# RWKV values turned to rows by token: from a run of their own in phase A into the state part's run of the unit before

## The chip, the cores and the metric

One NeuronCore of a Trainium2 chip runs the whole program. The metric is the device time of one execution in microseconds; lower is better. The engines are PE (TensorE), DVE (VectorE), ACT (ScalarE), POOL (GpSimd) and the DMA queue that SP issues to.

## The reference, cut to what matters

The reference is one layer of a hybrid decoder: 4,096 tokens of width 1,024 are normalised and projected once, the columns feed a gated linear attention group (GLA, 4 heads) and an RWKV-7 group (8 heads of size 64), and both outputs go through a gate, one output projection, a residual add and a last norm. The change touches the RWKV group alone:

```
def step(S, inp):                     # S is (value dim, key dim), one per head
    r_t, w_t, k_t, v_t, kk_t, a_t = inp
    sa = einsum('bhvk,bhk->bhv', S, -kk_t)
    S = S * w_t + sa * (kk_t * a_t) + v_t * k_t
    return S, einsum('bhvk,bhk->bhv', S, r_t)
mu, var = mean(y), var(y)             # per head, over its 64 values
y = (y - mu) * rsqrt(var + 64e-5) * ln_w + ln_b
out = (y + sum(r * k * r_k) * v) * silu(rg)
```

The values v_t are a shifted projection of the normalised input.

## The kernel before, in words

The tokens are cut into 8 blocks of 512 (`TB`). A block has four RWKV units, each with two heads, one on partitions 0 to 63 (`lo`) and one on 64 to 127 (`hi`); unit u is heads pair p = u % 4 of block b = u // 4, so there are 32 units. A unit has 8 chunks of 64 tokens (`NC`, `C`).

Work is written as generators (streams) that run side by side while the program is recorded: `stream_a` (projections and phase A of a unit, `rwkv_ab`), `stream_i` (the rest of the inverse of the unit's triangular matrix, `rwkv_i`), `stream_c` (the chain over the chunks and the output, `rwkv_c`), `rwkv_d` (the norm and the gate), and others for x, the weights, GLA and the output projection. Counters in `done` say which unit each has reached. What is recorded is a list of steps with their dependences. `forward` and `backward` (lines 270 to 356) are a list scheduler that runs over them several times with modelled durations, and the best order by its model is then issued. Every engine takes its instructions in that order. All instructions are therefore put on line 477 by the profile, and groups have to be told apart by tile names. The model of PE is `class Array` (lines 139 to 164): how long a matmul holds its tile of the array, and when PE can take the next one.

Most tiles are shared: `lend` (lines 206 to 218) enters a tile into a pool of its kind (PSUM banks; 512-wide f32 tiles in SBUF; and so on), and `settle` gives each use a place after the scheduling. So a name in the profile is that of the tile whose place was used. `bank` is any of 7 shared PSUM banks, `ch` the eighth; the values v may appear under `mgr`, `xr`, `r` or `go`. `c` is `c64` and keeps its name; `W` holds a unit's matrices.

The array can be used as smaller tiles. A matmul with K = 64 and 64 output partitions uses one quadrant, named by its rows (partitions of the inputs) and columns (partitions of the output). A f32 matmul appears in the trace as two MATMUL records with a weight load each, so 16 matmuls are x32.

Three groups of matmuls matter here.

- The **turn** (lines 1006 to 1014, at the end of phase A). v is stored with values on partitions and tokens along the row; `sv` wants tokens on partitions. Per chunk, two matmuls against `c64` (identity less 1/64, so the mean of each head is taken off too) turn the 64 x 64 pieces. Values of `lo` come out on `hi` and the other way round, so they use the two off-diagonal quadrants. 16 matmuls, then two ACT copies from PSUM into `sv`.
- The **chain** (lines 1051 to 1072): per chunk three dependent matmuls with copies between them, in the `ch` bank. Its first step reads `sv`.
- The **state part** of the output (lines 1073 to 1076): per chunk, `Ss` (state before the chunk) against W's third column block, `lo` to `lo` and `hi` to `hi`: the two diagonal quadrants, 16 matmuls. The part from the chunk's own values (lines 1077 to 1079) follows with K = 128 into the same bank.

`banks` holds the free PSUM banks; `need(st, n)` takes n of them for a stream and frees what the stream held.

Of the kernel before, what the change touches and what calls it, by code (L numbers as in the profile page):

```python
# [10 lines left out]
F32 = mybir.dt.float32  # L11
# [9 lines left out]
P = 128  # L21
# [3 lines left out]
C = 64  # L25
# [23 lines left out]
NC = TB // C  # L49
# [4 lines left out]
W_R, W_RK, W_RV, W_RG = 1, 5, 9, 13  # L54
# [29 lines left out]
def hymba_kernel(ctx, tc, xT, wt, wg, wo, wua, gup, pk, ck, out):  # L84
# [3 lines left out]
    NB = NT // TB  # L88

    one = ctx.enter_context(tc.tile_pool(name="one", bufs=1))  # L90
    wp = ctx.enter_context(tc.tile_pool(name="wp", bufs=1))
    big = ctx.enter_context(tc.tile_pool(name="big", bufs=1))
    un = ctx.enter_context(tc.tile_pool(name="un", bufs=1))
    rt = ctx.enter_context(tc.tile_pool(name="rt", bufs=1))
# [44 lines left out]
    class Array:  # L139
# [5 lines left out]
        def put(self, t, d, cols, tiles):  # L145
            r, c, f32 = tiles
            form = (r[1] - r[0], c[1] - c[0])
            q = [(i, j) for i in range(r[0], r[1]) for j in range(c[0], c[1])]
            turn = form != self.form
            t = max([t, self.free] + [self.tile.get(k, 0.0) for k in (self.tile if turn else q)]) + 0.09 * turn  # L150
            w, k = int(t / 3.413), self.clock
            if w > k[0]:
                k[:] = [w, 0.0, w == k[0] + 1 and k[1] >= 3060]
            k[1] += cols
            d *= 1 if k[2] else 2
            full = len(q) == 16
            if full and f32 == 2:
                load = 0.107 * (c[1] - c[0]) / 4
                d = max(0.0, load - self.one) + max(d / 2, load) + d / 2
            for k in q:  # L160
                self.tile[k] = t + (d if full or not f32 else 0.66 * d)
            self.form, self.f32, self.one = form, f32 > 0, d / max(f32, 1)
            self.free = t + (d if full or turn and f32 else d / 2 if f32 and form != (4, 1) else 0.014)
            return t, d

    array = Array()
# [25 lines left out]
    last, turn = [None, 0], [0]  # L192
# [288 lines left out]
    def after(*what):  # L481

        t = 0.0
        for x in what:
            if isinstance(x, tuple):
                r = ring.get((x[0], F32))
                for i in range(x[1] if r else 0):
                    y = r[1][(r[0] + i) % len(r[1])]
                    t = max([t] + [used.get(k, 0.0) for k in parts(y)])
            else:  # L490
                t = max([t] + [ready.get(k, (0.0, ""))[0] for k in parts(x)])
        return t + EL
# [24 lines left out]
    def sb(pool, shape, dt, tag, bufs=1):  # L517

        key = (tag, dt)
        if key not in ring:  # L520
            ring[key] = [0, [pool.tile(shape, dt, tag=f"{tag}_{i}", name=f"{tag}_{i}") for i in range(bufs)]]
        r = ring[key]
        t = r[1][r[0] % len(r[1])]
        r[0] += 1
        return t if pool is one else lend(t)
# [100 lines left out]
    hls = [wot(), wot()]  # L626
    wdr = [dr.tile([2, P, KT, P], F16, tag=f"wdr{i}", name=f"wdr{i}") for i in range(NWT + KT)]
    wgs = sb(one, [P, 2, KT, 32], F16, "wgs")
    scl = sb(one, [P, 40], F32, "scl")
    wosc = sb(one, [P, KT], F32, "wosc")  # L630
    woinv = sb(one, [P, KT], F32, "woinv")
    nwx = sb(one, [P, 10], F32, "nwx")
# [9 lines left out]
    def get_w(i, st="g"):  # L642
        if st != "o":
            got[st] += 1
        if i not in split_done:
            yield lambda: i in split_done
        if i in first:
            return first.pop(i)
        if st == "o":
            if done["W"] < NWT + KT:  # L650
                yield lambda: done["W"] == NWT + KT
            w = wot()
            w = [w[:, 0], w[:, 1]]
        else:
            w = pair(st)
        for a in range(2):
            D.dma_start(w[a], wdr[i][a])
        return w
# [182 lines left out]
    def proj(w, xs, st="g", kt=KT):  # L841
        yield after(w[0], xs[STEP - 1])
        ps = yield from need(st)
        for n, (a, c) in enumerate(((0, 0), (0, 1), (1, 0))):
            for k in range(kt):
                if k % STEP == 0 and n + k > 0:
                    yield after(w[a], xs[min(k + STEP, kt) - 1])
                count[st] += 1
                T.matmul(ps, lhsT=w[a][:, k, :], rhs=xs[k][:, c, :], start=(n == 0 and k == 0), stop=(n == 2 and k == kt - 1))
        return ps  # L850

    def shift(ps, j, o):

        a = sb(rt, [P, TB + 1], F32, "sa", NSA)
        S.copy(a[:, 0:1], carry[:, j:j + 1])
        S.activation(a[:, 1:TB + 1], ps, AF.Copy, scale=mu_s[:, j:j + 1])
        V.scalar_tensor_tensor(o, ps, omu_s[:, j:j + 1], a[:, 0:TB], ALU.mult, ALU.add)
        rel("r")
        S.copy(carry[:, j:j + 1], a[:, TB:TB + 1])
        return o  # L860
# [29 lines left out]
    def rwkv_ab(u, p, b, xs, LR):  # L890
# [11 lines left out]
        E = tA("E")  # L902
# [75 lines left out]
            D.dma_start(nb[32 * q:32 * q + 32, :, 32 * q:32 * q + 32],  # L978
                              td[:, :, NC * q:NC * q + NC].rearrange("m g c i -> (m g) c i"))

        v = shift((yield from proj((yield from get_w(W_RV + p, "r")), xs, "r")), 8 + p, tA("E"))
        yield lambda: done["C"] >= u - 1
        i = W_RG + p
        pg = yield from proj((yield from get_w(i, "r")), xs, "r")
# [4 lines left out]
        yield after(r)  # L989
        pst = yield from need("r")  # L990
        stat_mm(pst, bones, r)
        brow = sb(rt, [P, P], F32, "brow", 1)
        S.copy(brow, pst[:, 0:P])
        bv = tA("bv", 2)
        bcast(brow, 2, bv, "b")
# [7 lines left out]
        for i in range(2):  # L1003
            S.copy(bk[:, 4 * i:4 * i + 4, :], f4(pt[i]))
        rel("r")
        yield after(v)
        sv = sb(un, [P, NC, 2, 64], F32, "sv", 2)
        pv = (yield from need("r")).rearrange("p (c t) -> p c t", c=NC)
        for c in range(NC):
            t_ = slice(C * c, C * c + C)  # L1010
            T.matmul(pv[64:128, c, :], lhsT=v[0:64, t_], rhs=c64[0:64, :], start=True, stop=True)
            T.matmul(pv[0:64, c, :], lhsT=v[64:128, t_], rhs=c64[64:128, :], start=True, stop=True)
        S.copy(sv[64:128, :, 0, :], pv[64:128])
        S.copy(sv[0:64, :, 1, :], pv[0:64])
        units[u] = (W, nb, sv, bk, PC, bv, tg)
        done["A"] += 1

    def rwkv_i(nb):
# [20 lines left out]
            S.copy(nb[q0:q0 + 32, :, q0 + 32:q0 + 64], pl[q0:q0 + 32, 1])  # L1039
        rel("i")  # L1040

    def rwkv_c(p, b, mgt, st_):
        W, nb, sv, bkt, PC, bv, tg = st_
        yield after(nb, bkt, sv)

        st = Sst[p]
        S.copy(sv[lo, 0, 0, :], st[lo])
        V.tensor_copy(sv[hi, 0, 1, :], st[hi])
        S.copy(Ss[:, 0, :], st)
        dd = ((lo, 0), (hi, 1))  # L1050
        for c in range(NC):
            pc = pbank("ch").rearrange("p (a t) -> p a t", a=8)
            T.matmul(pc[:, 0:2, :], lhsT=W[:, c, 0:2, :].rearrange("p a t -> p (a t)"), rhs=sv[:, c], start=True, stop=True)
            us = sb(rt, [P, 64], F32, "us", 2)
            for q_, e in dd:
                S.copy(us[q_], pc[q_, e, :])
            if c > 0:
                for q_, e in dd:
                    S.copy(Ss[q_, c, :], sv[q_, c, e, :])
            psd = sb(rt, [P, 64], F32, "psd", 2)  # L1060
            yield after(us) + XL
            T.matmul(pc[:, 2, :], lhsT=nb[:, c, :], rhs=us, start=True, stop=True)
            for q_, e in dd:
                S.copy(sv[q_, c, e, :], pc[q_, 2, :])
            S.activation(psd, Ss[:, c, :], AF.Copy, scale=PC[:, c])
            yield after(sv) + XL
            T.matmul(pc[:, 4:6, :], lhsT=bkt[:, c, :], rhs=sv[:, c], start=True, stop=True)
            for q_, e in dd:
                dst = sv[q_, c + 1, e, :] if c < NC - 1 else st[q_]
                V.scalar_tensor_tensor(dst, pc[q_, 4 + e, :], PC[q_, c], psd[q_], ALU.mult, ALU.add)  # L1070
            if c < NC - 1:
                yield after(sv, ("ch", 1)) + XL
        py = (yield from need("y")).rearrange("p (c t) -> p c t", c=NC)
        for c in range(NC):
            for q_, e in dd:
                T.matmul(py[q_, c, :], lhsT=Ss[q_, c, :], rhs=W[q_, c, 2, :], start=c == 0, stop=False)
        for c in range(NC):
            for q_, e in dd:
                T.matmul(py[q_, c, :], lhsT=sv[:, c, e, :], rhs=W[:, c, 5 + e, :], start=False, stop=c == NC - 1)
        yield lambda: done["C"] == done["CC"]  # L1080
        y = sb(rt, [P, TB], F32, "cy")
        rs = sb(rt, [P, TB], F32, "crs")
        S.copy(y, py.rearrange("p c t -> p (c t)"))
        rel("y")
        S.activation(rs, y, AF.Square)
        done["CC"] += 1
        spawn(rwkv_d(p, b, mgt, y, rs, bv, tg), 2.5)
# [281 lines left out]
            D.dma_start(out[P * n:P * n + P, TB * b:TB * b + TB], part[n])  # L1369
        yield now[0]  # L1370

    done = dict.fromkeys(("A", "C", "G", "GE", "GV", "GG", "GH", "I", "CC", "O", "X", "W", "SU", "N"), 0)


    def norm_weight():
# [37 lines left out]
        D.dma_start(c64, ck[:, CK_C64:CK_C64 + 64])  # L1413


    units, hot = {}, []
    mgts = [[None] * KT + [sb(one, [P, KT], F32, f"mxs{b % 3}")] for b in range(NB)]

    def masks():
# [53 lines left out]

    def stream_c():
        for u in range(4 * NB):
            yield lambda: done["I"] > u
            yield from rwkv_c(u % 4, u // 4, mgts[u // 4], units.pop(u))

    def stream_p():
        for b in range(NB):  # L1480
# [110 lines left out]
```

## Time and profile before

| what | value |
|---|---|
| median of 3 runs | 2293.01 us (2292.14 to 2295.88) |
| the profiled execution | 2296.0 us |
| its span, first to last instruction | 2294.2 us |
| mean granted clock of TensorE | 0.99 |
| PE busy | 2219.4 us (97%), 20,200 MATMUL records |
| DVE, ACT, POOL busy | 1714.6, 1312.8, 893.2 us |
| HBM traffic | 276.97 MB read, 45.05 MB written |

Busy time of PE counts every record's modelled duration, overlapping ones once. For a run of small matmuls, the distance from its start to the start of the next row of the timeline is what it takes from PE. The queries used below are the page, the table by stretches of time (`windows`: length of the stretch, then busy time and instructions of PE, weight loads, DVE, ACT and POOL, then the granted clock, the share of DMA and GB/s), the groups of instructions with their shapes, and the timeline (start, length, engine, line, operation, output <- inputs, K*M of the array tile, output shape, records).

### The profile page before, as it was taken

The numbers are of one execution on the slowest core, as the hardware profiler recorded it, in microseconds if no ns is written. First come the engines' busy times: TensorE is split into PE (matmuls) and PEld (weight loads), VectorE is DVE, ScalarE is ACT, GpSimd is POOL, SyncE is SP. The second block draws the span as 40 slices with busy tenths as digits, with TensorE's granted clock in tenths as the row PEclk, the third lists the DMA queues.
The fourth block names the chain that finished last, engine by engine and source line by source line (L and its number), as shares of the span: only waits on it lengthen the run. The fifth ranks groups of instructions, "written<-read, shape, count | busy, mean of one in ns | idle before, by whom it ended". The sixth has DMA issues, their size and how long they took to land.

```text
span 2294.2 us, 54076 instructions
## 1 busy us (share of the span) xinstructions
PE 2219.4 (97%) x20200; PEld 1370.0 (60%) x20200; DVE 1714.6 (75%) x3863; ACT 1312.8 (57%) x3605; POOL 893.2 (39%) x2219
## 2 busy tenths in 40 slices
PE   6989999899999999999999999999999999999997
PEld 2546576456655666556665566655666566755663
DVE  8868979758685877777776596776877596776876
ACT  6657776555655546455663656555475464644562
POOL 4422534462155440554417253345315544044400
PEclk9999999999999999999999999999999999999998
DMA  7586454635444543456435344344534544344432
GB/s 248 184 239 209 129 180 147 182 106 164 124 129 141 158 139 107 118 154 182 117 101 167 101 158 131 109 132 131 170 103 133 168 132 134 112 119 117 114 116 70
DMA packets 275516, 325.59 MB, mean 142 GB/s; under 512 B 131716, under 2 KB 132916, under 8 KB 275252
## 3 DMA queue, kind: packets, MB, share of 16 engines
q1 hardware_dynamic: 275252, 322.13, 47.3%
q8 instruction: 158, 2.59, 0.5%
q14 instruction: 106, 0.87, 0.1%
HBM read 276.97 MB, written 45.05 MB: 140 GB/s over the span
## 4 chain that ended last, share of the span: by engine, by line
PE 79%; DVE 11%; DMA 5%; ACT 2%; issue 2%; POOL 1%; SPq 1%; DVEq 0%; ACTq 0%; POOLq 0%
PE bank L477 71%; PE ch L477 7%; DVE W L477 1%; DMA wdr<-wo 1%; DVE x L477 1%; DVE mgg L477 1%; POOL Tc L477 1%; SPq L477 1%; DVE mgr L477 1%; POOL tm L477 1%; DVE sv L477 1%; DMA x<-in_wt_dram 0%; ACT wo L477 0%; DMA mgg<-in_xT_dram 0%; DVE rgs L477 0%
## 5 line engine op out<-in xcount | busy, mean ns | idle before, releaser
L477 PE MATMUL bank<-x,wr 128*128 128x512 f16 x2992 | 758.3, 382 | 10.5 <-ACT x L477 4.6
L477 PE MATMUL bank<-x,wg 128*128 128x512 f16 x1808 | 466.3, 383 | 6.9 <-DVE wg L477 3.4
L477 PEld LDWEIGHTS <-wr 128*128 128x128 f16 x2992 | 290.6, 100 | 281.6 <-issue 21.5
L477 POOL TENSOR_TENSOR Tc<-Tc,tm 128x60 f32<-128x60 f32 (+24 forms) x961 | 373.9, 389 | 72.7
L477 PE MATMUL bank<-x,wo 128*128 128x512 f16 x1488 | 359.3, 379 | 0.0
L477 POOL TENSOR_TENSOR tm<-Tc,bk 128x60 f32<-128x60 f32 (+24 forms) x434 | 167.2, 385 | 376.9 <-DMA bk<-nd 198.9
L477 PEld LDWEIGHTS <-wg 128*128 128x128 f16 x1808 | 175.6, 100 | 175.9 <-issue 13.3
L477 PEld LDWEIGHTS <-wo 128*128 128x128 f16 x1488 | 143.8, 100 | 136.0 <-issue 3.0
L477 POOL TENSOR_TENSOR tm<-Tc,sv 128x66 f32<-128x66 f32 (+24 forms) x279 | 99.1, 355 | 276.0 <-DMA sv<-nd 163.4
L477 PEld LDWEIGHTS <-x 128*128 128x128 f16 x3120 | 189.6, 98 | 27.1 <-issue 8.0
L477 DVE COPY_PREDICATED W<-mc,bank 64x512 f32<-64x512 uint8 x256 | 180.3, 725 | 16.8 <-PE bank L477 12.8
L477 ACT COPY us<-ch 64x64 f32<-64x64 f32 x512 | 105.8, 207 | 108.5 <-PE ch L477 102.8
L477 ACT ACTIVATE sa<-bank,mu_s 128x512 f32<-128x512 f32 x104 | 71.5, 687 | 107.9 <-PE bank L477 106.7
L477 PE MATMUL bank<-wg,x 128*128 128x128 f16 x1632 | 116.4, 219 | 0.1
L477 POOL MEMSET Tc<- 32x8 f32 (+1 forms) x160 | 23.6, 148 | 234.7 <-DMA td<-Tc 193.2
L477 PEld LDWEIGHTS ch<-us,W 128*128 128x128 f32 x512 | 91.6, 190 | 35.5 <-ACT W L477 3.8
L477 PE MATMUL bank<-wr,x 128*128 128x128 f16 x1440 | 103.5, 219 | 0.0
L477 DVE SCALAR_TENSOR_TENSOR sv<-ch,PC,psd 64x64 f32<-64x64 f32 x154 | 43.5, 283 | 74.0 <-PE ch L477 70.3
L477 PE MATMUL ch<-us,W 128*128 128x64 f32 x512 | 90.6, 259 | 2.8 <-ACT W L477 2.0
L477 ACT ACTIVATE psd<-kf,PC 128x64 f32<-128x64 f32 x256 | 88.9, 347 | 6.7
L477 POOL TENSOR_TENSOR tm<-Tc,f 128x60 f32<-128x60 f32 (+24 forms) x124 | 46.5, 375 | 87.2 <-DMA f<-nd 66.1
L477 POOL TENSOR_TENSOR tm<-Tc,vt 128x60 f32<-128x60 f32 (+24 forms) x124 | 41.7, 336 | 83.3 <-ACT sv L477 54.9
(2014 smaller groups left out, 4207.8 us busy)
## 6 DMA issues: line engine op xcount, KB each, us to landing
wr<-wdr SPq DMA_DIRECT2D x250, 256.0 KB
wg<-wdr SPq DMA_DIRECT2D x190, 256.0 KB
wo<-wdr SPq DMA_DIRECT2D x128, 256.0 KB
x<-in_wt_dram SPq DMA_DIRECT2D x29, 512.0 KB
wdr<-wo SPq DMA_DIRECT2D x25, 512.0 KB
bk<-nd SPq DMA_DIRECT2D x60, 128.0 KB
mgg<-in_xT_dram SPq DMA_DIRECT2D x29, 256.0 KB
mgr<-in_xT_dram SPq DMA_DIRECT2D x24, 256.0 KB
```

The lines of the kernel that those rows point to most:

```text
L477: put(t0, self.name, d, lag, cols, tiles, tab, outs, ins, lambda: f(*[moved(x, ids) for x in a], **{k: moved(x, ids) for k, x in kw.items()}))
```

## The change

The turn leaves phase A. A new function `turned(u, state)` takes v of unit u, gets a PSUM bank for it, and runs the 16 matmuls. Where it is given `state`, it takes a second bank and issues, chunk by chunk, the two state matmuls of the unit before on the diagonal quadrants and then the two turns on the off-diagonal ones: 32 matmuls in one run. `rwkv_c` of unit u calls it for unit u + 1. Unit 0 has its turn alone ahead of the first chain, and unit 31 its state part alone. The two ACT copies into `sv` follow the run.

Beside that: phase A waits, in the recording, until the unit before has been turned (`done["V"]`), ahead of the projection of v; v gets a tile of its own (`v`) in the pool of 512-wide tiles, where it used that of `E`; `brow` uses the place of another 128-wide tile and `scl` is 32 wide where it was 40; and in the scheduler's model a f32 matmul on a quadrant holds its quadrant for the whole d, and PE can take the next one at once.

```
-            self.free = t + (d if full or turn and f32 else d / 2 if f32 and form != (4, 1) else 0.014)
+            self.free = t + (d if full or turn and f32 else d / 2 if f32 and form not in ((4, 1), (2, 2)) else 0.014)
...
-        v = shift((yield from proj((yield from get_w(W_RV + p, "r")), xs, "r")), 8 + p, tA("E"))
+        yield lambda: done["V"] >= u
+        v = shift((yield from proj((yield from get_w(W_RV + p, "r")), xs, "r")), 8 + p, tA("v"))
...
-        for c in range(NC):
-            t_ = slice(C * c, C * c + C)
-            T.matmul(pv[64:128, c, :], lhsT=v[0:64, t_], rhs=c64[0:64, :], start=True, stop=True)
-            T.matmul(pv[0:64, c, :], lhsT=v[64:128, t_], rhs=c64[64:128, :], start=True, stop=True)
-        S.copy(sv[64:128, :, 0, :], pv[64:128])
-        S.copy(sv[0:64, :, 1, :], pv[0:64])
...
+    def turned(u, state=None):
+        yield lambda: u in units
+        v = units[u][2]
+        yield after(v)
+        pv, *py = (yield from need("y", 2)) if state else [(yield from need("y"))]
+        pv = pv.rearrange("p (c t) -> p c t", c=NC)
+        sv = svs[u] = sb(un, [P, NC, 2, 64], F32, "sv", 2)
+        for c in range(NC):
+            t_ = slice(C * c, C * c + C)
+            if state:
+                state(py[0], c)
+            T.matmul(pv[hi, c, :], lhsT=v[lo, t_], rhs=c64[lo, :], start=True, stop=True)
+            T.matmul(pv[lo, c, :], lhsT=v[hi, t_], rhs=c64[hi, :], start=True, stop=True)
+        S.copy(sv[hi, :, 0, :], pv[hi])
+        S.copy(sv[lo, :, 1, :], pv[lo])
+        done["V"] += 1
+        return py
...
+        if u + 1 < 4 * NB:
+            py, = yield from turned(u + 1, state)
```

Since the scheduler's input changes, the whole order changes. Three places on PE show what the prediction speaks of. Rows with `c_0_99` are turns, those with `W` and `kf` state parts; the state is held in `Ss`, whose place is `kf`.

The first place is in block 2, units 8 and 9. Before, the turn of unit 9 stands by itself between an RWKV statistic and matmuls of the output projection, and the state part of unit 8 some 430 rows further on:

```order
L477 MATMUL bank_0_182<-qi_217,bones_98 32x128 x4
L477 MATMUL bank_0_183<-c_0_99,r_197 64x64 x16
L477 LDWEIGHTS wo_135
...
L477 MATMUL bank_0_182<-x_1_1_0_81,wo_135 128x512
L477 MATMUL bank_0_183<-W_0_130,kf_196 64x64 x16
L477 MATMUL bank_0_183<-W_0_130,bk_243 64x64 x16
```

In the changed kernel the same 32 matmuls alternate in one run, into two banks:

```order
L477 MATMUL ch_294<-f_0_214,W_0_130 128x128
L477 MATMUL bank_0_184<-W_0_130,kf_196 64x64 x2
L477 MATMUL bank_0_182<-c_0_99,Ss_132 64x64 x2
...
L477 MATMUL ch_294<-us_296,W_0_130 128x64
...
L477 MATMUL bank_0_184<-W_0_130,f_0_214 64x64 x16
```

One stretch of quadrant matmuls has gone from between the f16 matmuls. In the whole program PE had 57 stretches of 64 x 64 tiles and has 34.

The second place is the border between blocks 0 and 1, units 3 and 4. Before, the state part of unit 3 comes first and the turn of unit 4, of the next block, some 160 rows behind it:

```order
L477 MATMUL bank_0_181<-W_0_131,kf_196 64x64 x16
L477 MATMUL ch_294<-us_296,W_0_131 128x64
...
L477 MATMUL bank_0_184<-x_1_2_0_82,wg_227 128x512
L477 MATMUL bank_0_180<-c_0_99,gg_300 64x64 x16
L477 MATMUL bank_0_183<-W_0_131,bk_243 128x128
```

Now they are one run, which needs v of the next block's first unit; the last matmul of that projection stands 55 full f16 matmuls (128 x 512) ahead of the run:

```order
L477 MATMUL ch_294<-sv_278,W_0_131 128x128
L477 MATMUL bank_0_184<-W_0_131,kf_196 64x64 x2
L477 MATMUL bank_0_182<-c_0_99,xr_218 64x64 x2
...
L477 MATMUL ch_294<-us_296,W_0_131 128x64
L477 MATMUL bank_0_184<-W_0_131,sv_278 64x64 x16
```

What moved is the projection of v, to an earlier place; over all 31 merged runs the nearest one ends 43 such matmuls ahead.

The third place is the end, units 30 and 31. Before, the turn of unit 31 stands inside the chain of unit 30, and the last chain starts ahead of the state part of unit 30:

```order
L477 MATMUL bank_0_179<-c_0_99,gep_215 64x64 x16
...
L477 MATMUL ch_294<-f_0_214,W_0_131 128x128
...
L477 MATMUL ch_294<-us_295,W_0_131 128x64
...
L477 MATMUL bank_0_183<-W_0_130,kf_196 64x64 x16
L477 MATMUL ch_294<-f_0_214,vt_264 128x128
```

Now the last chain's first matmul, which reads the turned values, comes behind the merged run:

```order
L477 MATMUL bank_0_182<-W_0_130,kf_196 64x64 x2
L477 MATMUL bank_0_184<-c_0_99,ki_245 64x64 x2
...
L477 MATMUL ch_294<-bk_244,vt_264 128x128
...
L477 MATMUL bank_0_183<-Ta_280,W_0_131 32x32 x16
L477 MATMUL ch_294<-f_0_214,W_0_131 128x128
```

The order of run and chain has turned round there.

More of the change, by code (lines that the diff above doesn't have):

```diff
@@ L160, in put @@
             for k in q:
-                self.tile[k] = t + (d if full or not f32 else 0.66 * d)
+                self.tile[k] = t + (d if full or not f32 or form == (2, 2) else 0.66 * d)
             self.form, self.f32, self.one = form, f32 > 0, d / max(f32, 1)
-            self.free = t + (d if full or turn and f32 else d / 2 if f32 and form != (4, 1) else 0.014)
+            self.free = t + (d if full or turn and f32 else d / 2 if f32 and form not in ((4, 1), (2, 2)) else 0.014)
             return t, d
@@ L628, in hymba_kernel @@
     wgs = sb(one, [P, 2, KT, 32], F16, "wgs")
-    scl = sb(one, [P, 40], F32, "scl")
+    scl = sb(one, [P, 32], F32, "scl")
     wosc = sb(one, [P, KT], F32, "wosc")
@@ L991, in rwkv_ab @@
         stat_mm(pst, bones, r)
-        brow = sb(rt, [P, P], F32, "brow", 1)
+        brow = sb(rt, [P, P], F32, "nya")
         S.copy(brow, pst[:, 0:P])
@@ L1005, in rwkv_ab @@
         rel("r")
-        yield after(v)
-        sv = sb(un, [P, NC, 2, 64], F32, "sv", 2)
-        pv = (yield from need("r")).rearrange("p (c t) -> p c t", c=NC)
-        for c in range(NC):
-            t_ = slice(C * c, C * c + C)
-            T.matmul(pv[64:128, c, :], lhsT=v[0:64, t_], rhs=c64[0:64, :], start=True, stop=True)
-            T.matmul(pv[0:64, c, :], lhsT=v[64:128, t_], rhs=c64[64:128, :], start=True, stop=True)
-        S.copy(sv[64:128, :, 0, :], pv[64:128])
-        S.copy(sv[0:64, :, 1, :], pv[0:64])
-        units[u] = (W, nb, sv, bk, PC, bv, tg)
+        units[u] = (W, nb, v, bk, PC, bv, tg)
         done["A"] += 1
@@ L1040, in rwkv_i, with rwkv_c @@
         rel("i")
-    def rwkv_c(p, b, mgt, st_):
-        W, nb, sv, bkt, PC, bv, tg = st_
+    def turned(u, state=None):
[15 more added lines that the diff above has]
+        return py
+    def rwkv_c(u, p, b, mgt, st_):
+        W, nb, _, bkt, PC, bv, tg = st_
+        sv = svs.pop(u)
         yield after(nb, bkt, sv)
@@ L1072, in rwkv_c, with state @@
                 yield after(sv, ("ch", 1)) + XL
-        py = (yield from need("y")).rearrange("p (c t) -> p c t", c=NC)
-        for c in range(NC):
+        def state(py, c):
             for q_, e in dd:
-                T.matmul(py[q_, c, :], lhsT=Ss[q_, c, :], rhs=W[q_, c, 2, :], start=c == 0, stop=False)
+                T.matmul(py[q_, C * c:C * c + C], lhsT=Ss[q_, c, :], rhs=W[q_, c, 2, :], start=c == 0, stop=False)
+        if u + 1 < 4 * NB:
+            py, = yield from turned(u + 1, state)
+        else:
+            py = yield from need("y")
+            for c in range(NC):
+                state(py, c)
+        py = py.rearrange("p (c t) -> p c t", c=NC)
         for c in range(NC):
@@ L1370, in out_last @@
         yield now[0]
-    done = dict.fromkeys(("A", "C", "G", "GE", "GV", "GG", "GH", "I", "CC", "O", "X", "W", "SU", "N"), 0)
+    done = dict.fromkeys(("A", "C", "G", "GE", "GV", "GG", "GH", "I", "CC", "O", "X", "W", "SU", "N", "V"), 0)
     def norm_weight():
@@ L1413, in setup @@
         D.dma_start(c64, ck[:, CK_C64:CK_C64 + 64])
-    units, hot = {}, []
+    units, svs, hot = {}, {}, []
     mgts = [[None] * KT + [sb(one, [P, KT], F32, f"mxs{b % 3}")] for b in range(NB)]
@@ L1475, in stream_c @@
         for u in range(4 * NB):
+            if u == 0:
+                yield from turned(0)
             yield lambda: done["I"] > u
-            yield from rwkv_c(u % 4, u // 4, mgts[u // 4], units.pop(u))
+            yield from rwkv_c(u, u % 4, u // 4, mgts[u // 4], units.pop(u))
     def stream_p():
```

## The prediction

> **What bounds the kernel now.** I read the page first, then the table by stretches, then the groups by shape, and last the timeline of PE around the moved matmuls. The page:
>
> ```profile
> span 2294.2 us, 54076 instructions
> PE 2219.4 (97%) x20200; PEld 1370.0 (60%) x20200; DVE 1714.6 (75%) x3863; ACT 1312.8 (57%) x3605; POOL 893.2 (39%) x2219
> ...
> PE   6989999899999999999999999999999999999997
> ...
> PEclk9999999999999999999999999999999999999998
> ...
> PE 79%; DVE 11%; DMA 5%; ACT 2%; issue 2%; POOL 1%; SPq 1%; DVEq 0%; ACTq 0%; POOLq 0%
> ```
>
> PE is busy 97% of the span, at full clock, and holds 79% of the chain that ended last. The table by stretches shows where the rest is:
>
> ```profile
> 0.00:100.00 100.00, 75.72 (x436) 39.05 (x437) 81.98 (x226) 65.34 (x116) 40.26 (x86) 0.93 0.70 224
> 2200.00:2300.00 100.00, 77.04 (x642) 44.39 (x640) 61.22 (x140) 40.33 (x124) 0.00 (x0) 0.92 0.29 92
> ```
>
> ```profile
> 200.00:2200.00 2000.00, 1977.92 (x18394) 1233.72 (x18395) 1497.53 (x3291) 1140.69 (x3223) 815.60 (x2039) 1.00 0.46 136
> ```
>
> In the 2,000 us of the body PE idles 22 us, so what PE is spared there the span is spared, unless a new wait takes it. The head and the last 94 us are not PE's.
>
> **What a run costs PE.** Two islands, a turn and a state part, each between f16 matmuls:
>
> ```profile
> 561.81 0.38 PE L477 MATMUL bank<-x,wg 128*128 128x512 f16 x1
> 562.12 1.15 PE L477 MATMUL bank<-c,go 64*64 64x64 f32 x32
> 563.20 0.49 PE L477 MATMUL ch<-sv,W 128*128 128x128 f32 x2
> ...
> 1013.48 0.38 PE L477 MATMUL bank<-x,wo 128*128 128x512 f16 x1
> 1013.79 1.15 PE L477 MATMUL bank<-W,kf 64*64 64x64 f32 x32
> 1014.87 5.35 PE L477 MATMUL bank<-x,wo 128*128 128x512 f16 x24
> 1020.06 0.38 PE L477 MATMUL ch<-sv,W 128*128 128x128 f32 x2
> ```
>
> A f16 matmul in a stream takes (1020.06 - 1014.87) / 24 = 0.216 us. So each run takes 1.08 us from its start to the next row, and with the change of tile ahead of it (562.12 - 561.81 - 0.216 = 0.09) the island is 1.17 us. Both kinds use two quadrants and cost the same.
>
> Whether four quadrants run at once is the question on which the change stands. The trace has the answer by accident: at eight of the 32 places PE's order has a turn and a state part back to back, on opposite quadrants, and PE lets them overlap for a moment at the border. One of the eight:
>
> ```profile
> 529.57 0.97 PE L477 MATMUL bank<-c,E 64*64 64x64 f32 x26
> 530.33 0.27 PE L477 MATMUL bank<-W,kf 64*64 64x64 f32 x2
> 530.38 0.28 PE L477 MATMUL bank<-c,E 64*64 64x64 f32 x3
> 530.43 0.22 PE L477 MATMUL bank<-W,kf 64*64 64x64 f32 x1
> 530.44 0.22 PE L477 MATMUL bank<-c,E 64*64 64x64 f32 x1
> 530.44 0.22 PE L477 MATMUL bank<-W,kf 64*64 64x64 f32 x1
> 530.49 0.22 PE L477 MATMUL bank<-c,E 64*64 64x64 f32 x1
> 530.49 0.22 PE L477 MATMUL bank<-W,kf 64*64 64x64 f32 x1
> 530.50 0.22 PE L477 MATMUL bank<-c,E 64*64 64x64 f32 x1
> 530.50 0.98 PE L477 MATMUL bank<-W,kf 64*64 64x64 f32 x27
> 531.41 0.43 PE L477 MATMUL ch<-us,W 128*128 128x64 f32 x2
> ```
>
> On two quadrants 26 records start in 0.76 us, one per 29 ns. From 530.33 to 530.50, where both kinds are in flight, 11 start in 0.17 us: one per 15.5 ns, nearly twice the rate. 32 records at 29 ns are 0.93 us, so a run of 1.08 carries 0.15 us that don't scale. The back-to-back pair takes 531.41 - 529.57 = 1.84 us.
>
> A merged run has 64 records: 64 x 15.5 ns + 0.15 = **1.14 us**, about what one of the two costs today. This sets the term, and the low end would be 1.08 (perfect overlap), the high end 64 x 29 ns + 0.15 = 2.01 us (none).
>
> The Trainium skill, "TensorE: Matmul & The Clock Gate" (Part 3: Packing small matmuls, The mechanism), says that a weight load overlaps matmuls in flight only where the row group differs. It speaks against this change: of four quadrants two share each row group, so their loads would wait, and the merged run would be nearer to 2.01 us. The trace has a run with two column tiles on the same rows:
>
> ```profile
> 1021.03 1.15 PE L477 MATMUL bank<-W,f 128*64 128x64 f32 x32
> 1022.11 2.06 PE L477 MATMUL bank<-W,vt 64*128 64x128 f32 x32
> ```
>
> It takes 1022.11 - 1021.03 = 1.08 us, the same as with two row groups. So sharing rows costs nothing that shows, and the sum stays with 1.14.
>
> **The change part by part.**
>
> *The turn merged.* 31 turns join a state part (unit 0's stays alone). The 23 that were islands (32 less eight, less unit 0): 1.17 + 1.08 - 1.14 = 1.11 us each, 25.5 us. The eight back to back: 1.84 - 1.14 = 0.70 each, 5.6 us. Sum **-31 us**. Each removed island also spares what the next row pays for restarting; I count nothing for that.
>
> *The copies into `sv`.* Two per unit, unchanged in number. They now follow the merged run, and the next unit's chain needs them, where before they could be made any time ahead:
>
> ```profile
> 2215.56 0.58 ACT L477 COPY f<-bank 64x512 f32<-64x512 f32 x1
> ```
>
> So run and copies, 1.14 + 2 x 0.58 = 2.3 us, now lie between the last steps of one chain and the first of the next. In the body other streams fill PE meanwhile, and the cover is the stock of projection matmuls. At the end there is none: the last chain starts behind the merged run of unit 30 and its copies. I take **+2 us** for that, bounds 0 and 4.
>
> *The wait in the recording, v's own tile, the smaller tables.* `done["V"]` orders only the recording; what runs is the scheduler's order, in which every merged run has v's projection far ahead (43 full f16 matmuls at the nearest, 43 x 0.216 = 9.3 us of PE). The shift that makes v of a projection takes ACT and DVE one after the other, as in this one:
>
> ```profile
> 2208.48 0.69 ACT L477 ACTIVATE sa<-bank,mu_s 128x512 f32<-128x512 f32 x1
> ...
> 2209.20 0.75 DVE L477 SCALAR_TENSOR_TENSOR gep<-bank,omu_s,sa 128x512 f32<-128x512 f32 x1
> ```
>
> From 2208.48 to 2209.95 that is 1.5 us, so no stall: 0. Two banks held at once for 1.1 us and then released one after the other: 0, of 7. No DMA is added, and the weights of the v projection are fetched as often as before. The scheduler draws a new order altogether; with 22 us of PE idle in the body I allow it 8 us either way and count 0.
>
> **Sum:** -31 + 2 = -29 us, rounded with the restarts not counted to -30. The profiled execution took 2296.0 us (span 2294.2), the median is 2293.0: **2263 us** against the median.
>
> **The rivals.**
>
> *No overlap (10%).* PE starts one record per 29 ns whatever the quadrants. Then a merged run is 2.01 us, an island saves 1.17 + 1.08 - 2.01 = 0.24, 23 of them 5.5 us, back-to-back pairs nothing, less 2 at the end: about 2289 us, within 0.2%. Against it stand the eleven starts in 0.17 us, and a run of 32 x 32 tiles:
>
> ```profile
> 1027.87 0.69 PE L477 MATMUL bank<-Ta,W 32*32 32x32 f32 x32
> 1028.49 0.43 PE L477 MATMUL bank<-mgr,bones 128*32 128x128 f32 x8
> ```
>
> 0.62 us for 32 records is 19.4 ns each, the 0.15 included. For it: the burst is short, eleven records, and might be a queue emptying. The same page of the Trainium skill (Wait — 56ns, not 53.3ns?) gives a floor of about 25 ns between starts however small the matmul; by that a merged run would be 1.75 us and the kernel about 2283 (an estimate from that figure). The 19.4 ns row lies below the floor.
>
> *The chain binds (14%).* At the end of a block chains follow each other closely:
>
> ```profile
> 347.25 1.15 PE L477 MATMUL bank<-W,kf 64*64 64x64 f32 x32
> ...
> 378.39 1.15 PE L477 MATMUL bank<-W,kf 64*64 64x64 f32 x32
> ```
>
> From unit 2's state part to unit 3's it is 31 us. If the 2.3 us between chains stay uncovered at eight such places, 8 x 2.3 = 18 us are given back: 2281, or 2272 if half. Against: PE is busy all through there.
>
> *Slower: the next block's v comes late (8%).* The state part of a block's last unit now waits for v of the next block's first unit. Before, that could come later. The state part at 378.39 above is unit 3's, and the turn of unit 4 is:
>
> ```profile
> 399.34 1.15 PE L477 MATMUL bank<-c,gg 64*64 64x64 f32 x32
> ```
>
> It ran 21 us after unit 3's state part. If y of unit 3, the merged block and with it the output projection slip by that, PE runs dry at seven borders. It decides from (30 + 4.6) / 7 = 4.9 us of new idle time per border; at 8 us each it is 2263 + 56 = 2319 us. Against: in the new order v's projection ends 55 f16 matmuls, 12 us, ahead of that very run, and PE has GLA and output matmuls to put in between.
>
> **How the numbers follow.** My forecast (2253 to 2273) has 68%, the three rivals 10, 14 and 8. The range takes in the chain's case in full, with 3 us above it for the new order: **2252 to 2284**. It leaves out the no-overlap case and the slow one. A measurement of this kernel tells 0.2%, 4.6 us, from no change. Faster by more: 68 + 14 and half of the first rival, 87%; within: 5%; slower: 8%.
>
> **What would show it.** Right: runs of 64 x 64 tiles, 64 records in 1.05 to 1.2 us from start to next row; 31 of them; PE busy in all some 30 us lower; PE's share still 97%. If a run takes 1.6 to 2.0 us, the quadrants don't overlap. If PE's idle time in the body rises above 22 us by some 10 or more, and its waits name ACT or DVE results of `sv` or of the shift of v, the chain or the border has taken the gain. If PE's busy time is down and the last 94 us are longer by more than 4, it is the end.

## The result, and the profile after

The changed kernel takes 2262.09 us (median of 4 runs, 2258.5 to 2265.23) against 2293.82 us before in the same comparison. The ratio is 0.9861, with a 95% interval of 0.9843 to 0.9878: 1.4% faster. The profiled execution took 2263.05 us.

The page of the changed kernel, the lines that answer to those of before:

```profile
span 2261.3 us, 54230 instructions
...
PE 2181.7 (96%) x20200; PEld 1344.8 (59%) x20200; DVE 1715.6 (76%) x3863; ACT 1306.3 (58%) x3605; POOL 865.8 (38%) x2219
...
PE   6989999999999999999999999999999999999997
...
PE 80%; DVE 7%; DMA 6%; POOL 3%; ACT 2%; issue 1%; SPq 1%; DVEq 0%; ACTq 0%; POOLq 0%
```

PE does the same 20,200 records in 37.7 us less. The span is 32.9 us shorter, so PE's idle time (span less busy) has gone from 74.8 to 79.6 us. What PE was spared has nearly all come out of the span.

One merged run on the timeline, the one that holds the state part of unit 6 and the turn of unit 7:

```profile
588.29 0.38 PE L477 MATMUL bank<-x,wg 128*128 128x512 f16 x1
588.60 0.27 PE L477 MATMUL bank<-W,kf 64*64 64x64 f32 x2
588.62 0.27 PE L477 MATMUL bank<-c,xr 64*64 64x64 f32 x2
588.71 0.22 PE L477 MATMUL bank<-W,kf 64*64 64x64 f32 x2
588.72 0.23 PE L477 MATMUL bank<-c,xr 64*64 64x64 f32 x2
...
589.53 0.23 PE L477 MATMUL bank<-W,kf 64*64 64x64 f32 x2
589.54 0.22 PE L477 MATMUL bank<-c,xr 64*64 64x64 f32 x2
589.70 0.51 PE L477 MATMUL bank<-W,sv 128*64 128x64 f32 x10
```

Two records of each kind start together, and from 588.71 to 589.53 the next four follow every 58.6 ns (14 steps): one record per 14.6 ns, half the 29 ns of two quadrants. The 64 records take 589.70 - 588.60 = 1.10 us, what 32 took before.

To see where in the program the time went, the state parts of units 1 and 29 serve as marks. Before:

```profile
271.24 1.15 PE L477 MATMUL bank<-W,kf 64*64 64x64 f32 x32
...
2143.48 0.33 PE L477 MATMUL bank<-W,kf 64*64 64x64 f32 x2
```

and in the changed kernel:

```profile
267.25 0.27 PE L477 MATMUL bank<-W,kf 64*64 64x64 f32 x2
...
2114.34 0.27 PE L477 MATMUL bank<-W,kf 64*64 64x64 f32 x2
```

The head is 4.0 us shorter, the body between the marks 25.1 us (1872.2 to 1847.1), and the end behind unit 29 3.7 us (150.7 to 147.0).

### The profile page after: what moved, and what is told of

The parts are those of the page before. It is cut to its first block, busy times and chain, and to the rows that moved or that the text cites. A ratio compares the mean times of both kernels' runs of the same rounds, so it can differ in the third digit from the quotient of the medians.

```text
span 2261.3 us, 54230 instructions
## 1 busy us (share of the span) xinstructions
PE 2181.7 (96%) x20200; PEld 1344.8 (59%) x20200; DVE 1715.6 (76%) x3863; ACT 1306.3 (58%) x3605; POOL 865.8 (38%) x2219
## 4 chain that ended last, share of the span: by engine, by line
PE 80%; DVE 7%; DMA 6%; POOL 3%; ACT 2%; issue 1%; SPq 1%; DVEq 0%; ACTq 0%; POOLq 0%
PE bank L477 72%; PE ch L477 7%; DMA wdr<-wo 2%; POOL tm L477 1%; POOL Tc L477 1%; SPq L477 1%; DVE W L477 1%; DVE mgr L477 1%; DMA wr<-wdr 0%; DVE f L477 0%; DVE mgg L477 0%; ACT wo L477 0%; DVE x L477 0%; DMA bk<-nd 0%; DVE sv L477 0%
## 5 line engine op out<-in xcount | busy, mean ns | idle before, releaser
L477 PE MATMUL bank<-x,wr 128*128 128x512 f16 x2480 | 623.7, 383 | 7.8 <-ACT x L477 4.2
L477 PE MATMUL bank<-x,wg 128*128 128x512 f16 x2320 | 590.0, 380 | 2.4 <-DVE wg L477 1.2
L477 PEld LDWEIGHTS <-wr 128*128 128x128 f16 x2480 | 242.9, 101 | 238.6 <-issue 18.1
L477 PEld LDWEIGHTS <-wg 128*128 128x128 f16 x2320 | 223.3, 100 | 206.3 <-issue 7.2
L477 POOL TENSOR_TENSOR tm<-Tc,sv 128x60 f32<-128x60 f32 (+24 forms) x372 | 134.8, 362 | 338.0 <-DMA sv<-nd 123.7
L477 POOL TENSOR_TENSOR tm<-Tc,bk 128x60 f32<-128x60 f32 (+24 forms) x341 | 128.1, 376 | 224.3 <-DMA bk<-nd 155.9
L477 PEld LDWEIGHTS <-x 128*128 128x128 f16 x3120 | 189.6, 99 | 29.3 <-issue 9.7
L477 PE MATMUL bank<-wr,x 128*128 128x128 f16 x2400 | 162.7, 220 | 5.2 <-DMA wr<-wdr 5.0
L477 POOL TENSOR_TENSOR tm<-Tc,vt 128x60 f32<-128x60 f32 (+24 forms) x186 | 65.4, 352 | 147.2 <-DMA vt<-nd 123.6
L477 ACT COPY kf<-sv 64x64 f32<-64x64 f32 x154 | 37.1, 241 | 43.3 <-DVE sv L477 38.8
L477 DVE SCALAR_TENSOR_TENSOR f<-ch,PC,psd 64x64 f32<-64x64 f32 x98 | 27.7, 283 | 44.1 <-PE ch L477 41.9
```

The source lines that it names most:

```text
L477: put(t0, self.name, d, lag, cols, tiles, tab, outs, ins, lambda: f(*[moved(x, ids) for x in a], **{k: moved(x, ids) for k, x in kw.items()}))
```

## The experiments

Theory 1 is that of the prediction: four quadrants work at once, a merged run costs no more than one of its halves, and the gain is that PE time. Theory 2 is that the gain is in what else the change does: fewer islands, a new order, the edited model. Every kernel was compared with the kernel before on the same chip; across comparisons, differences are taken from the ratios (0.001 is 2.3 us). All together, the by columns kernel with the one execution that it had, with PE's idle time as span less busy, and the three stretches of the profiled execution between the marks above:

| kernel | median us | ratio to before (95%) | PE busy | idle | head | body | end |
|---|---|---|---|---|---|---|---|
| before | 2293.8 | | 2219.4 | 74.8 | 271.2 | 1872.2 | 150.7 |
| changed | 2262.1 | 0.9861 (0.9843 to 0.9878) | 2181.7 | 79.6 | 267.2 | 1847.1 | 147.0 |
| unwoven | 2274.1 | 0.9907 (0.9887 to 0.9927) | 2199.9 | 69.7 | 269.9 | 1853.6 | 146.1 |
| by rows | 2316.8 | 1.0084 (1.0060 to 1.0107) | 2222.2 | 90.4 | 279.6 | 1876.8 | 156.2 |
| by columns | 2306.1 | 1.0055 (one execution, no interval) | 2210.6 | 93.7 | 272.9 | 1875.7 | 155.7 |
| old model | 2272.9 | 0.9895 (0.9878 to 0.9911) | 2187.4 | 83.8 | 276.2 | 1842.9 | 152.1 |
| model alone | 2287.4 | 0.9955 (0.9938 to 0.9973) | 2213.9 | 72.0 | 278.1 | 1860.0 | 147.8 |
| apart | 2301.5 | 1.0036 (1.0025 to 1.0047) | 2217.5 | 81.3 | 269.2 | 1888.3 | 141.2 |
| borders | 2274.4 | 0.9916 (0.9899 to 0.9934) | 2195.5 | 79.3 | 270.6 | 1859.1 | 145.1 |
| pairs | 2272.9 | 0.9900 (0.9876 to 0.9925) | 2188.1 | 83.6 | 285.2 | 1832.8 | 153.7 |
| before, look-ahead 0.6 | 2282.5 | 0.9952 (0.9933 to 0.9971) | 2212.7 | 66.8 | 265.0 | 1863.6 | 150.9 |
| changed, look-ahead 0.6 | 2260.8 | 0.9859 (0.9843 to 0.9876) | 2182.7 | 77.0 | 273.9 | 1832.3 | 153.5 |
| before, look-ahead 0.8 | 2288.1 | 0.9979 (0.9967 to 0.9991) | 2208.0 | 78.4 | 268.0 | 1870.9 | 147.5 |
| changed, look-ahead 0.8 | 2263.6 | 0.9864 (0.9843 to 0.9885) | 2179.2 | 82.7 | 273.8 | 1839.3 | 148.8 |

**Unwoven.** The merged run with two quadrants at a time:

```
         for c in range(NC):
-            t_ = slice(C * c, C * c + C)
             if state:
                 state(py[0], c)
+        for c in range(NC):
+            t_ = slice(C * c, C * c + C)
             T.matmul(pv[hi, c, :], lhsT=v[lo, t_], rhs=c64[lo, :], start=True, stop=True)
```

> The merged run keeps its place, but the 16 state matmuls come first and the 16 turns behind them, so that two quadrants work at a time. Theory 1 (four quadrants at once make the gain): the run goes from 1.09 to 1.84 us, as the back-to-back pairs of before, 31 x 0.75 = 23 us more than the changed kernel, 2285 us. Theory 2 (the gain is the islands saved and the new order): no change, 2262 us within 6.

At 27 of the 31 places the run is as slow as theory 1 says; at the other four the order put other work between the halves, so that they are two islands again. On the timeline of this kernel, state records first, then turns, with the short overlap at the border:

```profile
511.97 0.97 PE L477 MATMUL bank<-W,kf 64*64 64x64 f32 x26
512.73 0.27 PE L477 MATMUL bank<-c,mgg 64*64 64x64 f32 x2
...
512.90 0.98 PE L477 MATMUL bank<-c,mgg 64*64 64x64 f32 x27
513.81 0.43 PE L477 MATMUL ch<-us,W 128*128 128x64 f32 x2
```

It takes 513.81 - 511.97 = 1.84 us. PE's busy time is 18.2 us above the changed kernel, of the 23 expected. But by the ratios (0.9907 and 0.9861) the kernel is only 10.6 us slower than the changed one, half of what theory 1 gave, since PE idles 9.9 us less (69.7 for 79.6). The granted clock has a part in that: in its profiled execution the changed kernel had PE busy for some 40 us at a granted clock of 0.50, this one for 22, and a f16 matmul in a stream takes 0.427 us there in place of 0.216. With that time counted half, an estimate, PE works about 27 us more here than in the changed kernel, where 27 x 0.75 and four islands at 1.16 make 25. The price of the run is settled, its worth in the span isn't.

This kernel also shows how much comes without four quadrants: it is still 0.93%, 21 us, faster than before. By the prediction's prices, the islands saved are worth at most 23 x (1.17 + 1.08 - 1.84) = 9.4 us of that; the rest is what one new order can do, or stays open.

**By rows.** The same matmuls in the order of their rows:

```
-        for c in range(NC):
...
+        for i, (q_, o_) in enumerate(((lo, hi), (hi, lo))):
+            for c in range(NC):
+                if state:
+                    state(py[0], c, [(q_, i)])
+                T.matmul(pv[o_, c, :], lhsT=v[q_, C * c:C * c + C], rhs=c64[q_, :], start=True, stop=True)
```

> Same 32 matmuls in the merged run, but first the two quadrants on the lower rows (state and turn of the lower head), then the two on the upper rows. Quadrants independent: each half runs two quadrants, as fast as any two, 1.84 us per run, 2285 us. If quadrants that share their rows hold each other up (loads wait for matmuls in flight on the same rows): well over 1.84 us, up to 3.6 us if one record has to end before the next begins, 2290 to 2340 us.

At 2317 us this looks like the second case, and it is not. Most runs take 2.73 us, and the timeline shows where:

```profile
748.52 0.27 PE L477 MATMUL bank<-W,kf 64*64 64x64 f32 x1
748.52 0.27 PE L477 MATMUL bank<-c,rgs 64*64 64x64 f32 x1
...
749.26 0.22 PE L477 MATMUL bank<-W,kf 64*64 64x64 f32 x1
749.27 0.22 PE L477 MATMUL bank<-c,rgs 64*64 64x64 f32 x1
...
749.79 0.28 PE L477 MATMUL bank<-W,kf 64*64 64x64 f32 x2
750.64 0.27 PE L477 MATMUL bank<-c,rgs 64*64 64x64 f32 x1 [0.57 <-ACT f L477]
```

The two quadrants that share the lower rows start side by side, and the next pair follows some 58 ns later: 748.52 to 749.26 are 26 records, one per 29 ns, the pace of any two quadrants. Behind 749.79 the next row comes 0.85 us later; by then the first four turns of the second half have already started. On ACT, at that place:

```profile
750.01 0.58 ACT L477 COPY f<-bank 64x512 f32<-64x512 f32 x1 [2.56 <-PE bank L477]
```

The copy of the finished half of the turned bank ends at 750.59, and PE goes on at 750.64: the fifth turn into the other half of the bank waits for a semaphore that this copy raises. The program holds that wait; whether the chip would need it, no run tells. So shared rows cost nothing that shows: 28 of the 31 runs lost by a wait, 19 of them 1.84 + 0.9 = 2.73 us, nine 2.8 to 4.2. Three runs took 1.84. The waits explain some 28 x 0.9 = 25 us; by the ratios the kernel is 41 us slower than the unwoven one, and what makes the rest is not shown.

**By columns.** As by rows, with `pv[q_]` and `v[o_]`: first the two quadrants that share their output columns.

> The merged run with first the two quadrants on the lower columns (outputs on partitions 0 to 63), then the two on the upper ones. Quadrants independent: each half at one record per 29 ns, as by rows; between the halves the wait for an ACT copy from the turned bank, some 0.9 us, as by rows, run 2.7 us, about 2315 us. If quadrants that share columns hold each other up: a pitch well over 29 ns within a half.

The one execution took 2306 us, below the 2315 expected, and five of its 31 runs took 1.84 us, without the wait. In the others the same picture:

```profile
747.75 0.27 PE L477 MATMUL bank<-W,kf 64*64 64x64 f32 x1
747.75 0.27 PE L477 MATMUL bank<-c,rgs 64*64 64x64 f32 x1
...
748.49 0.22 PE L477 MATMUL bank<-W,kf 64*64 64x64 f32 x1
748.50 0.22 PE L477 MATMUL bank<-c,rgs 64*64 64x64 f32 x1
...
749.87 0.27 PE L477 MATMUL bank<-c,rgs 64*64 64x64 f32 x1 [0.57 <-ACT f L477]
```

26 records in 0.74 us, and behind them the wait for ACT. Two quadrants run at the same pace, whether they share rows, columns or neither.

**Pairs.** Woven by two chunks in place of one: four state matmuls, four turns, and so on.

```
+        for c0 in range(0, NC, 2):
+            for c in range(c0, c0 + 2):
+                if state:
+                    state(py[0], c)
+            for c in range(c0, c0 + 2):
+                t_ = slice(C * c, C * c + C)
+                T.matmul(pv[hi, c, :], lhsT=v[lo, t_], rhs=c64[lo, :], start=True, stop=True)
+                T.matmul(pv[lo, c, :], lhsT=v[hi, t_], rhs=c64[hi, :], start=True, stop=True)
```

> The run woven by two chunks: four state matmuls, then four turns, and so on, instead of two and two. If PE's queue looks ahead over some eight records (as the border of the back-to-back pairs suggests, where about five records start early): four quadrants still overlap most of the time, run 1.1 to 1.3 us, 2262 to 2268 us. If it starts records strictly in order: each group of eight records waits for its own two quadrants, run 1.84 us, about 2275 to 2285 us.

```profile
1062.78 0.27 PE L477 MATMUL bank<-W,kf 64*64 64x64 f32 x2
1062.81 0.27 PE L477 MATMUL bank<-c,mgr 64*64 64x64 f32 x2
1062.89 0.22 PE L477 MATMUL bank<-W,kf 64*64 64x64 f32 x2
1062.91 0.23 PE L477 MATMUL bank<-c,mgr 64*64 64x64 f32 x2
...
1063.92 1.15 PE L477 MATMUL bank<-W,sv 128*64 128x64 f32 x32
```

In the program eight state records stand ahead of the first turn. On the chip the first turns start 0.03 us after the first two state records, ahead of the other six. PE starts what finds its quadrant free, out of the written order, and the run takes 1063.92 - 1062.78 = 1.14 us. The kernel's time came out above the 2262 to 2268 us expected (2273, or 2271 by the ratio). The run explains 31 x 0.05 = 1.6 us. Three of the four executions took 2272 to 2274 us at a mean granted clock of 0.986 or 0.987, the fourth 2263.4 at 0.990; so the clock may make the difference as well as the order, and no run separates them here. The next experiments show what the order does.

**Old model** and **model alone.** The changed kernel with the scheduler's two lines as they were, and the kernel before with the two new lines:

```
-                self.tile[k] = t + (d if full or not f32 or form == (2, 2) else 0.66 * d)
+                self.tile[k] = t + (d if full or not f32 else 0.66 * d)
...
-            self.free = t + (d if full or turn and f32 else d / 2 if f32 and form not in ((4, 1), (2, 2)) else 0.014)
+            self.free = t + (d if full or turn and f32 else d / 2 if f32 and form != (4, 1) else 0.014)
```

> The changed kernel with the scheduler's model of the quadrants as it was, so that it takes a merged run for some 1.7 us. Theory 1: the run still takes 1.09 us, only the order is drawn anew, 2262 us within 6. Rival (the model's edit places the work better and makes part of the gain): 2268 to 2285 us.

> The kernel before with the model's edit alone; no turn is moved. Theory 1: no gain, 2293 us within 6, which also shows how far a new drawing of the order moves the time. Rival (the model's edit makes the gain or part of it): 2262 to 2285 us.

The first missed theory 1's 6 us, the second stands at its edge (2287.4 for 2287). By the ratios both moved further. The old model costs the changed kernel 8 us (0.9895 for 0.9861), with merged runs of 1.09 us all the same, and the new one alone gains 0.45%, 10 us, on the kernel before, with islands of 1.08 us. Either the model's edit is worth some 10 us, or an order drawn anew moves the time by that much.

**Apart.** The changed kernel, model and all, with nothing merged:

```
-        if u + 1 < 4 * NB:
-            py, = yield from turned(u + 1, state)
-        else:
-            py = yield from need("y")
-            for c in range(NC):
-                state(py, c)
+        py = yield from need("y")
+        for c in range(NC):
+            state(py, c)
...
-            if u == 0:
-                yield from turned(0)
+            yield from turned(u)
```

The wait ahead of v's projection is one unit looser (`u - 1`).

> The changed kernel with its tile for v, its smaller tables and its model, but the turn of a unit in a run by itself ahead of that unit's chain, and the state part alone, so nothing is merged. Theory 1 (the gain is the merged run with four quadrants): the gain is gone but for the drawing of the order, and 64 runs of 1.08 us are back, 2287 us (as the model's edit alone) to 2293, within 6. Theory 2 (the rest of the change makes the gain): 2262 to 2270 us.

2301.5 us, slower than before, and 2.5 us beyond the upper end of what was expected. Without the merge nothing is left of the gain, though the model's edit is in. Theory 2 falls as far as the model and the rest of the change go; its fewer islands come with the merge itself, and unwoven is the only run that has them without four quadrants at once. It also puts the model alone in its place: this kernel has the same edited model and is 0.8%, 19 us, slower than that one.

**Borders.** Seven merges undone, between the last unit of a block and the first of the next:

```
-        if u + 1 < 4 * NB:
+        if (u + 1) % 4:
             py, = yield from turned(u + 1, state)
...
-            if u == 0:
-                yield from turned(0)
+            if u % 4 == 0:
+                yield from turned(u)
```

> The changed kernel with seven of its 31 merges undone, those at the borders of blocks (unit 4b+3 with 4b+4). Theory 1: 7 x 1.16 = 8 us lost, 2270 us within 6. Rival (waiting there for v of the next block costs more than the merge gains): 2262 us or less.

2274.4 us, by the ratios 12.6 us above the changed kernel, with 13.8 us more PE time, where 8 were expected. An order drawn anew can make the difference, but nothing says that the borders cost: the rival's 2262 us or less is excluded, and in the changed kernel, as in the four others with all merges woven, PE is never idle just ahead of a merged run. That v of the next block is needed earlier is no cost that shows.

**Two other orders.** To tell what a new order does by itself, the look-ahead of the scheduler was set to 0.6 and 0.8, in both kernels:

```
-                start, end = forward(backward(end), 0.7)
+                start, end = forward(backward(end), 0.6)
```

> The kernel before with another setting of the scheduler's look-ahead (0.6 for 0.7), so that the same work is drawn in another order. Both theories: 2293 us within 8 either way, the spread of an order.

> The changed kernel under the same other setting (0.6). Theory 1 (the merged run is worth some 30 us whatever the order): 30 us below the kernel before at 0.6, within 10; in the body, from the second to the 30th state part, 28 x 1.16 = 32 us less. Rival (the change is worth some 20 us, as the two other kernels with woven runs gave, and 10 us were luck of the order): 20 us below, the body 20 to 25 us less.

> The kernel before with the look-ahead at 0.8: a second other order. 2293 us within 8.

> The changed kernel at 0.8. Theory 1: 30 us below the kernel before at 0.8, within 10, the body 32 us less. Rival: 20 us below, the body 20 to 25 us less.

From the pages, the kernel before and the changed one at 0.6:

```profile
span 2279.5 us, 54127 instructions
...
PE 2212.7 (97%) x20200; PEld 1371.0 (60%) x20200; DVE 1708.3 (75%) x3863; ACT 1308.8 (57%) x3605; POOL 878.0 (39%) x2219
```

```profile
span 2259.7 us, 54241 instructions
...
PE 2182.7 (97%) x20200; PEld 1346.2 (60%) x20200; DVE 1718.9 (76%) x3863; ACT 1305.7 (58%) x3605; POOL 865.5 (38%) x2219
```

and at 0.8:

```profile
span 2286.4 us, 54167 instructions
...
PE 2208.0 (97%) x20200; PEld 1368.8 (60%) x20200; DVE 1717.8 (75%) x3863; ACT 1308.2 (57%) x3605; POOL 880.8 (39%) x2219
```

```profile
span 2261.9 us, 54210 instructions
...
PE 2179.2 (96%) x20200; PEld 1343.6 (59%) x20200; DVE 1701.8 (75%) x3863; ACT 1303.7 (58%) x3605; POOL 875.6 (39%) x2219
```

PE is spared 30.0 and 28.8 us of busy time, and idles 10.2 and 4.3 us more.

The change is worth 31.7, 21.7 and 24.6 us in the three orders (medians), and the kernel before spreads over 11 us from order to order, more than the 8 expected; the changed kernel spreads over 3. Its own order was the poorest of the three of the kernel before. In the body the three pairs give 25.1, 31.3 and 31.6 us less, 29.3 in the mean. The 28 x 1.16 = 32 us expected there is too much: in each of the three kernels before, eight of the 28 places are back to back and spare 0.75, so the merged runs spare 20 x 1.16 + 8 x 0.75 = 29.2 us. What is missing in the totals lies in the head: -4.0, +8.9 and +5.8 us. The end is even (-3.7, +2.6, +1.3). Theory 1 has the body right; the rival is nearer in the total, at 0.6 above all.

## Why the prediction was right, point by point

**The place and the bound.** PE's body was the bound, and still is. Right.

**Four quadrants at once.** The merged run was put at 1.14 us from eleven records at the border of a back-to-back pair. Measured: 1.09 to 1.10 us in 28 of 31 runs (one was split by another run, and two took 1.9 us, at a granted clock of 0.50 in their stretches). By that the term is 23 x 1.16 + 8 x 0.75 = 32.7 us in place of 31. The trap was whether the eleven records were a queue emptying; the merged run itself keeps their pace over 64 records, and pairs and unwoven show that four quadrants at work make it.

The sum of 31 us holds two things: 23 islands saved, at 0.41 us each 9.4 us, and 31 runs on four quadrants in place of two, at 0.70 us 21.7. With PE's busy time at a granted clock of 0.50 counted half, PE works 2198.4 us in the mean of the five kernels without a merge (before, model alone, apart, look-ahead 0.6 and 0.8), 2189.1 unwoven and 2166.7 in the mean of the five with all 31 woven (changed, old model, pairs, look-ahead 0.6 and 0.8). So the islands gave 9.3 us and the four quadrants 22.4. This is an estimate: its middle term is one kernel, with four places not merged, and single orders lie up to 5 us from their mean.

**The rules that spoke against it.** By the Trainium skill's page "TensorE: Matmul & The Clock Gate" (The mechanism) weight loads overlap matmuls in flight only where the row group differs; by rows, two quadrants on the same rows keep 29 ns, as two on different ones do. By the floor of about 25 ns between starts that the same page of the Trainium skill gives (Wait — 56ns, not 53.3ns?) the run would have been 1.75 us, an estimate from that figure; the records start every 14.6 ns. In both the trace of before had the better answer.

**What hides and what doesn't.** Idle time in the new order was counted at 0, with 8 us allowed either way. This is the step that was off. Over the five kernels without a merge PE is busy 2214.3 us in the mean and idle 74.7; over the five woven ones 2183.8 and 81.3. PE is spared 30.5 us, as forecast, and 6.6 of them return as waiting, so 23.9 are left in the span. The 6.6 is loose: single kernels idle 66.8 to 81.3 us without a merge and 77.0 to 83.9 with it. That the first pair shows 32 is the order: of the profiled spans, that of the kernel before lies 5 us above the mean of its five, and that of the changed kernel 4 us below the mean of its own. So the forecast was right in its mechanism and lucky in how close it came: 7 us of idle time that was not counted and some 8 us by which the orders favoured the pair cancel.

**The end.** +2 us was counted for the last chain behind the merged run. The three pairs give -3.7, +2.6 and +1.3, nothing that stands out, so no run shows the term. The head was counted at 0 and gave +3.6 in the mean. Unit 0's output now waits for v of unit 1 at a time when PE isn't the bound, which would explain it, but no kernel undid that merge alone. Over all kernels without a merge the head is 265 to 278 us, with all woven 267 to 285: it stays open.

**The rivals.** No overlap: refuted by the run itself. The chain binds: at most 18 us were put on it, and 6.6 us of waiting came back. Of that 4.2 us lie in the body, and the idle time just ahead of chain matmuls there goes from 7.4 to 9.3 us in the means, so the chain has some 2 us at most by this count; the rest is spread over other rows. Late v at the borders: refuted, undoing those merges made it slower, and PE never waits at a merged run.

## What to carry to other kernels

Look at which tiles of the array a run of small matmuls uses: a run that leaves half of them empty can take a second one of the same shape for next to nothing (1.09 us for 1.08), if the data is ready, and the weave need not be exact (1.14 us in pairs). Here the two wrote different banks; no run tried one. Where a scheduler draws the whole order from its input, an edit can move the time by some 10 us here whatever it is for, so an edit of that size is judged over several orders, by the busy time of the bound engine and by its body, not by one pair of times. And of time spared on a bound engine expect a part back as waiting, here 13% to 34% in the three pairs.

## What the runs showed of the hardware that had not been expected

PE starts f32 records of different quadrants out of the written order: in pairs, turns start ahead of six state records that stand before them. Four quadrants at once start a record every 14.6 ns, and with two quadrants at work (on a diagonal, on the same rows, on the same columns) the pace is the same 29 ns. What held the runs by rows up was not the array: a semaphore wait for one ACT copy of 0.58 us made a run 0.9 us longer, more than the 0.75 that the weave gains.
